# Sixteen tokens of the dense expert layer take fetched rows, and expert matrices move two key blocks at a time

## The chip, the cores and the metric

The kernel runs on one core of a Trainium2 chip. Its time is device microseconds (us) of that core, the median of several runs of one whole launch. A profile of one execution gives the durations. TensorE (PE) does the matrix products, VectorE (DVE) and ScalarE (ACT) the elementwise work, GpSimd (POOL) issues the gathers, SyncE (SP) issues most transfers.

## The reference, cut to what matters

One layer with a token mixer and a channel sublayer, 512 latent tokens of width 1024. The change is in the channel sublayer, a retrieval over 128 x 128 = 16384 experts of one neuron each (8 heads, 16 experts per head and token):

```python
def block(t):                                   # t: 128 tokens
    q = (t @ w_query).reshape(128, 8, 2, 128)
    v1, i1 = top_k(q[:, :, 0] @ k1.T, 16)       # first keys
    v2, i2 = top_k(q[:, :, 1] @ k2.T, 16)       # second keys
    top_s, pos = top_k(all 256 sums v1 + v2, 16)
    idx = take(i1 * 128 + i2, pos)
    g = softmax(top_s)
    act = gelu(einsum('thkd,td->thk', expert_u[idx], t))
    return einsum('thk,thkd->td', g * act, expert_v[idx])
x = layer_norm(ALPHA * x + g2 * y, ln_gamma[1], ln_beta[1])
```

Everything is float32. The kernel writes each float32 factor as a high and a low part and takes three products (`mm3`).

## The kernel before, in words

The mixer comes first and ends at about 490 us. Then class `Peer` treats the 512 tokens in two ways.

Blocks 0 to 2 (384 tokens) are dense. For each of the 128 first keys, `hidden` (L1118) loads the 128 experts of that key as a slice of `uT` (512 KB), splits it into `uh` and `ul` (ACT, DVE), multiplies it with all 384 tokens (24 matmuls with 384 columns, tile `pH`) and takes the GELU. `gated` (L1141) multiplies by the gates, which are zero for experts that were not chosen, and splits the product into `ah` and `al`. `rows` (L1157) loads and splits the slice of `v` (`vh`, `vl`). `combine` (L1161) adds the key's part to the six accumulators `y` (18 matmuls with 512 columns).

Block 3 (128 tokens) is fetched: `fetched` (L1170) gathers per token the rows of `u` and `v` that were chosen, 256 gathers of 512 KB, issued by POOL up to five ahead (`LOOK`). A row of `u` is one DVE instruction with a dot product per token (tile `scr`), a row of `v` one that adds to `yg`.

`run` (L1219) sets the order. In the top stage the queries are made (`pq`), DVE picks the experts (`pick_heads`, `picks`), and gates are built by one-hot products (`gate_block`: DVE tiles `oh` and `ohg`, PE tile `pG`) and written to DRAM (`Gd`). Meanwhile `more` calls `hidden` so that 64 keys are done by the end; 56 of the results go to DRAM (`Hd`). One fetched row stands with each of the 48 gate groups (`ROWS[0]`). In the main stage each step makes `hidden` for one of the other 64 keys and `combine` for one key, with 2.75 fetched rows (`ROWS[1]`). Then `combine` goes on alone. The last five keys (`TAIL`) are held back: their `combine` is done block by block, so that `finish` of a block (DVE: residual and layer norm, L1203) can stand beside the `combine` of the next.

Each engine runs its list in a fixed order, written by a scheduler when the kernel is built; where `manual_schedule` is on, DVE or POOL keeps the order of the source. An instruction that waits holds up all behind it on its engine.

Of the kernel before, what the change touches and what calls it, by code (L numbers as in the profile page):

```python
# [19 lines left out]
D = 1024  # L20
# [11 lines left out]
class Net:  # L32
# [231 lines left out]
    def to_rows(self, js, pool, ps, tag):  # L264
# [4 lines left out]
        r = pool.tile([24, 128], F32, name="mrows")[0:n]  # L269
        nc.scalar.activation(r, p, AF.Copy)  # L270
        nc.gpsimd.dma_start(self.m2d[0, js, :], r)
# [398 lines left out]
    def out_proj(self, pool, mpool, pers, ps, last):  # L670
# [55 lines left out]
        def norms(b):  # L726
# [12 lines left out]
            self.h2[b] = h2  # L739
            for g in range(2):  # L740
# [118 lines left out]

def together(gens):  # L860
# [19 lines left out]
def host_layout(i):  # L880
# [10 lines left out]
    for p in range(2):  # L891
# [20 lines left out]
        "uT": i["peer_u"][0].reshape(128, 128, 8, 128).transpose(0, 3, 2, 1),  # L912
# [5 lines left out]
class Peer:  # L918
# [86 lines left out]
    def picks(self, w, b):  # L1005
# [23 lines left out]
        key = self.key = w.tile([128, 2, 8, 16], F32, name="key")  # L1029
        yield  # L1030
        for s in range(2):
            oh = w.tile(full, BF, name="oh", bufs=2)
# [73 lines left out]
    def load_split(self, rpool, pool, src, tag, bufs=2, far=True, rbufs=2, lbufs=None):  # L1106
        nc = self.nc
        raw = rpool.tile([128, 8, 128], F32, name=tag + "r", bufs=rbufs)
        nc.sync.dma_start(raw, src)
        hi = pool.tile([128, 8, 128], F32R, name=tag + "h", bufs=bufs)  # L1110
        lo = pool.tile([128, 8, 128], F32R, name=tag + "l", bufs=lbufs or bufs)
        nc.scalar.activation(hi, raw, AF.Copy)  # L1112
        eng = nc.gpsimd if far else nc.vector
        sub = eng.tensor_tensor(lo, raw, hi, op=OP.subtract)  # L1114
        if not far:
            self.mark = sub.ins
        return hi, lo

    def hidden(self, n, pool, ring, ps):

        uh, ul = self.load_split(pool, pool, self.a["uT"][n], "u", 3, False, 3, 2)
        p = ps.tile([128, self.TD], F32, name="pH")
        for k in range(8):
            self.n.mm3(p, uh[:, k, :], ul[:, k, :], self.hh[:, k, :self.TD], self.hl[:, k, :self.TD], k == 0, k == 7)
        kept = not self.AHEAD <= n < self.AHEAD + self.SPILL
        r = ring.tile([128, self.TD], F32, name="gel" if kept else "gels", bufs=self.AHEAD + 1 if kept else 3)
        act = self.nc.scalar.activation(r, p, AF.Gelu_apprx_tanh)  # L1127
        if kept:
            self.gel[n] = r
        else:  # L1130
            self.nc.sync.dma_start(self.Hd[n - self.AHEAD], r)
        return act

    def back(self, n, ring):

        if self.AHEAD <= n < self.AHEAD + self.SPILL:
            r = self.gel[n] = ring.tile([128, self.TD], F32, name="gel", bufs=self.AHEAD + 1)
            self.nc.sync.dma_start(r, self.Hd[n - self.AHEAD])

    def gated(self, n, pool, vpool, bufs, mark=None):  # L1140

        nc = self.nc
        NG = self.TD // self.GT
        if n % self.GN == 0:
            self.Gn = pool.tile([128, NG, self.GN, self.GT], F32, name="Gn", bufs=2)
            nc.sync.dma_start(self.Gn, self.Gd[:, :, n:n + self.GN, :].rearrange("g m n t -> m g n t"))
        g = self.gel.pop(n)
        g3 = g.rearrange("p (g t) -> p g t", t=self.GT)
        with self.tc.issue_after(mark) if mark else ExitStack():
            nc.vector.tensor_tensor(g3, g3, self.Gn[:, :, n % self.GN, :], op=OP.mult)  # L1150
        ah = vpool.tile([128, self.TD], F32R, name="ah", bufs=bufs)
        al = vpool.tile([128, self.TD], F32R, name="al", bufs=bufs)
# [4 lines left out]
    def rows(self, n, pool, vpool, bufs, far=False, rbufs=2):  # L1157

        return self.load_split(pool, vpool, self.a["v"][n * 128:(n + 1) * 128].rearrange("e (k c) -> e k c", k=8), "v", bufs, far, rbufs)

    def combine(self, n, b, ops, halves=(0, 1)):  # L1161
# [236 lines left out]
```

## Time and profile before

| | |
|---|---|
| Runs | 1752.32, 1756.19, 1761.13 us; median 1756.19 |
| The profiled execution | 1752.71 us, of it 1750.9 us between first and last instruction |
| Busy share | PE 97%, DVE 83%, ACT 47%, POOL 24% |
| `pH` matmuls | 3 x 1024, 384 columns |
| `y` matmuls | 3 x 768, 512 columns |
| Granted TensorE clock | 0.987 of full speed |

How to read it: a matmul's own duration (some 340 or 395 ns) is longer than its distance to the next, since matmuls overlap in the pipeline, so the cost of one is read from the distance between starts. The mean busy shares run over stages with different limits; the rows below are by stage.

### The profile page before, as it was taken

To read this page: it belongs to the slowest core of one execution; us is meant where nothing else is said; L and a number is where in the kernel's file an instruction comes from. 1 tells how busy PE (TensorE), PEld (TensorE's weight loads), DVE (VectorE), ACT (ScalarE), POOL (GpSimd) and SP (SyncE) were. 2 spreads that over 40 slices of the span, in tenths; PEclk is the share of its full clock that TensorE was granted. 3 is DMA by queue.
4 is the path that set the end of the run, shared out by engine and by line. 5 is a ranking of instruction groups with operands and counts; after the bars stand their busy time and mean duration, and the time that the engine had idled before them with its cause. 6 is when DMAs were issued, how large, how long until landed. Compare 5 with 4: busy or idle time off the path is not lost. (4 is left out here: it accounts for less than half of the span.)

```text
span 1750.9 us, 28102 instructions
## 1 busy us (share of the span) xinstructions
PE 1692.9 (97%) x10440; PEld 1477.1 (84%) x10440; DVE 1446.2 (83%) x2917; ACT 829.9 (47%) x1412; POOL 416.6 (24%) x294
## 2 busy tenths in 40 slices
PE   6999999989999999999999999999999999999996
PEld 3888777877788999999998999999999998888884
DVE  6689888877989999999996887877877786777767
ACT  4667677655233356676663333333333333333341
POOL 0000000000033012258323454443444442111000
PEclk8999999989999999999999999999999999999998
DMA  8345445143322358989999999989989989999852
GB/s 318 127 145 163 130 142 183 53 158 135 133 74 72 97 172 304 332 298 311 347 332 364 374 338 329 334 304 332 333 301 336 326 287 333 336 347 282 275 194 96
DMA packets 175499, 431.10 MB, mean 246 GB/s; under 512 B 15137, under 2 KB 78977, under 8 KB 171266
## 3 DMA queue, kind: packets, MB, share of 16 engines
q1 hardware_dynamic: 137234, 290.87, 48.8%
q0 software_dynamic: 37552, 136.35, 22.3%
q8 instruction: 81, 1.33, 0.3%
q10 hardware_dynamic: 576, 2.10, 0.3%
q14 instruction: 56, 0.46, 0.1%
HBM read 380.48 MB, written 48.78 MB: 245 GB/s over the span
## 5 line engine op out<-in xcount | busy, mean ns | idle before, releaser
L139 PE MATMUL pH<-hh,uh 128*128 128x384 f32 x1024 | 350.1, 342 | 1.0 <-ACT gels L1127 1.0
L141 PE MATMUL pH<-hh,ul 128*128 128x384 f32 x1024 | 347.7, 340 | 1.6 <-DVE ul L1114 1.6
L140 PE MATMUL pH<-hl,uh 128*128 128x384 f32 x1024 | 346.9, 339 | 0.0
L139 PE MATMUL y<-vh,ah 128*128 128x512 f32 x768 | 302.5, 395 | 2.6 <-ACT ah L1153 2.6
L141 PE MATMUL y<-vh,al 128*128 128x512 f32 x768 | 301.8, 395 | 0.0
L140 PE MATMUL y<-vl,ah 128*128 128x512 f32 x768 | 301.4, 392 | 0.0
L1114 DVE TENSOR_TENSOR vl<-vr,vh 128x1024 fp32r<-128x1024 f32 x128 | 156.7, 1224 | 152.4 <-ACT vh L1112 152.0
L1183 POOL DMA_INDIRECT erow<-in_u_dram,ix x128 | 189.6, 1481 | 368.7 <-DVE scr L1192 214.6
L1183 POOL DMA_INDIRECT erow<-in_v_dram,ix x128 | 188.9, 1476 | 323.8 <-DVE yg L1200 181.1
L1112 ACT ACTIVATE vh<-vr 128x1024 fp32r<-128x1024 f32 x128 | 135.1, 1057 | 199.8 <-issue 128.8
L1153 ACT ACTIVATE ah<-gel 128x384 fp32r<-128x384 f32 x128 | 66.8, 524 | 272.7 <-DVE gel L1150 267.9
L139 PEld LDWEIGHTS pH<-hh,uh 128*128 128x128 f32 x1024 | 192.3, 188 | 3.9 <-ACT gels L1127 1.4
L140 PEld LDWEIGHTS pH<-hl,uh 128*128 128x128 f32 x1024 | 192.7, 188 | 2.7
L141 PEld LDWEIGHTS pH<-hh,ul 128*128 128x128 f32 x1024 | 192.3, 188 | 2.6 <-DVE ul L1114 2.4
L1112 ACT ACTIVATE uh<-ur 128x1024 fp32r<-128x1024 f32 x128 | 135.0, 1056 | 117.6 <-PE pH L140 71.2
L141 PEld LDWEIGHTS y<-vh,al 128*128 128x128 f32 x768 | 144.7, 188 | 34.4
L139 PEld LDWEIGHTS y<-vh,ah 128*128 128x128 f32 x768 | 144.4, 188 | 33.3 <-ACT ah L1153 2.9
L140 PEld LDWEIGHTS y<-vl,ah 128*128 128x128 f32 x768 | 144.5, 188 | 30.6
L1114 DVE TENSOR_TENSOR ul<-ur,uh 128x1024 fp32r<-128x1024 f32 x128 | 156.0, 1219 | 16.5 <-PE pH L141 13.6
L1200 DVE SCALAR_TENSOR_TENSOR yg<-erow,act,yg 128x1024 f32<-128x1024 f32 x127 | 162.4, 1279 | 0.1
L1192 DVE SCALAR_TENSOR_TENSOR scr<-erow,h 128x1024 bf16<-128x1024 f32 x128 | 156.1, 1219 | 0.0
L139 PE MATMUL pc<-hTh,wh 128*128 128x512 f32 (+1 forms) x304 | 109.5, 360 | 0.3 <-ACT G L379 0.3
(381 smaller groups left out, 3033.8 us busy)
## 6 DMA issues: line engine op xcount, KB each, us to landing
ur<-in_uT_dram SPq DMA_DIRECT2D x128, 512.0 KB
vr<-in_v_dram SPq DMA_DIRECT2D x128, 512.0 KB
Gd<-stage SPq DMA_DIRECT2D x24, 1024.0 KB
Gn<-Gd SPq DMA_DIRECT2D x16, 1536.0 KB
wraw<-in_w_cf_dram SPq DMA_DIRECT2D x24, 512.0 KB
wada<-in_w_ada_dram SPq DMA_DIRECT2D x48, 256.0 KB
Hd<-gels SPq DMA_DIRECT2D x56, 192.0 KB
gel<-Hd SPq DMA_DIRECT2D x56, 192.0 KB
```

What stands on the lines that cost most here:

```text
L139: mm(out, lh, rh, start=start, stop=False)
L140: mm(out, lh, rl, start=False, stop=False)
L141: mm(out, ll, rh, start=False, stop=stop)
L1112: nc.scalar.activation(hi, raw, AF.Copy)
L1114: sub = eng.tensor_tensor(lo, raw, hi, op=OP.subtract)
L1153: nc.scalar.activation(ah, g, AF.Copy)
L1183: nc.gpsimd.indirect_dma_start(out=e, out_offset=None, in_=a[src], in_offset=bass.IndirectOffsetOnAxis(ap=self.ix[:, j:j + 1], axis=0))
L1192: nc.vector.scalar_tensor_tensor(scr, e, 1.0, h2, op0=OP.mult, op1=OP.mult, accum_out=dots[:, j:j + 1])
L1200: nc.vector.scalar_tensor_tensor(y, e, act[:, j:j + 1], y, op0=OP.mult, op1=OP.add)
```

## The change

Five parts. (1) The dense product with `u` leaves out the last 16 of the 384 tokens (`SH`, `TU` = 368), so `pH` matmuls have 368 columns. (2) For these 16 tokens the dot products come from fetched rows: the 16 tokens x 128 chosen experts are spread over 128 partitions, 16 more gathers with index `ixs`, each with one DVE instruction (`sdots`). The GELU of the dots is multiplied into the gates of the 16 tokens, before the gate groups of block 2 are built, so that the gate matrix itself holds gate times activation and `gated` copies it. To have the indices in time `picks` of block 2 moves ahead of that of block 3. (3) `hidden`, `gated`, `rows` and `back` take two first keys at a time: loads of 1 MB, 8 KB in a row per partition, where there were 512 KB with 4 KB. (4) Buffers follow: `TAIL` is two pairs, `AHEAD` four pairs, `finish` holds its two tiles as one. (5) Fetched rows are done from `picks` of block 3 on; `ROWS[2]` is 0.75, counted twice per pair.

The diff, cut to its core:

```diff
+            if b == 2:
+                nc.gpsimd.dma_start(self.h2d, h2[128 - Peer.SH:128, :])
...
-        "uT": i["peer_u"][0].reshape(128, 128, 8, 128).transpose(0, 3, 2, 1),
+        "uT": i["peer_u"][0].reshape(64, 2, 128, 8, 128).transpose(0, 4, 1, 3, 2),
+        "vd": i["peer_v"][0].reshape(64, 2, 128, 8, 128).transpose(0, 2, 1, 3, 4),
...
+    SH = 16
+    TU = TD - SH
-    AHEAD = 8
-    SPILL = 56
+    AHEAD = 4
+    SPILL = 28
-    ROWS = (1.0, 2.75, 0.6)
+    ROWS = (1.0, 2.75, 0.75)
-    TAIL = 5
+    TAIL = 2
...
+    def load_split(self, pool, src, tag, bufs):
+        raw = pool.tile([128, 2, 8, 128], F32, name=tag + "r", bufs=2)
         nc.sync.dma_start(raw, src)
+        for e in range(2):
+            hi, lo = (pool.tile([128, 8, 128], F32R, name=tag + i, bufs=bufs) for i in "hl")
+            nc.scalar.activation(hi, raw[:, e], AF.Copy)
+            self.mark = nc.vector.tensor_tensor(lo, raw[:, e], hi, op=OP.subtract).ins
...
     def hidden(self, n, pool, ring, ps):
-        uh, ul = self.load_split(pool, pool, self.a["uT"][n], "u", 3, False, 3, 2)
-        p = ps.tile([128, self.TD], F32, name="pH")
-        for k in range(8):
-            self.n.mm3(p, uh[:, k, :], ul[:, k, :], self.hh[:, k, :self.TD], self.hl[:, k, :self.TD], k == 0, k == 7)
+        u = self.load_split(pool, self.a["uT"][n], "u", 3)
+        for e in range(2):
+            uh, ul = u[e]
+            p = ps.tile([128, TU], F32, name="pH")
+            for k in range(8):
+                self.n.mm3(p, uh[:, k, :], ul[:, k, :], self.hh[:, k, :TU], self.hl[:, k, :TU], k == 0, k == 7)
+            self.nc.scalar.activation(r[:, e, :TU], p, AF.Gelu_apprx_tanh)
...
+        nc.scalar.activation(g4[:, :, NU:], gates[:, :, NU:], AF.Copy)
         with self.tc.issue_after(mark) if mark else ExitStack():
-            nc.vector.tensor_tensor(g3, g3, self.Gn[:, :, n % self.GN, :], op=OP.mult)
+            nc.vector.tensor_tensor(g4[:, :, :NU], g4[:, :, :NU], gates[:, :, :NU], op=OP.mult)
+        ah = vpool.tile([128, 2, self.TD], F32R, name="ah", bufs=bufs)
+        al = vpool.tile([128, 2, self.TD], F32R, name="al", bufs=bufs)
...
+        order = [("s", j) for j in range(SH)]
+        order += [(src, j) for j0 in range(0, 128, 16) for src in "uv" for j in range(j0, j0 + 16)]
...
+            if src == "s":
+                nc.vector.scalar_tensor_tensor(e, e, 1.0, y, op0=OP.mult, op1=OP.mult, accum_out=sdots[:, j:j + 1])
+                if j == SH - 1:
+                    nc.scalar.activation(sdots, sdots, AF.Gelu_apprx_tanh)
+                    for q in range(128 // SH):
+                        nc.scalar.dma_start(act[128 - SH:128, q * SH:(q + 1) * SH], sdots[q * SH:(q + 1) * SH, :])
+            elif src == "u":
+                nc.vector.scalar_tensor_tensor(e, e, 1.0, h2, op0=OP.mult, op1=OP.mult, accum_out=dots[:, j:j + 1])
+                if j == 15:
+                    g = self.g[96:128, 2].rearrange("p h k -> p (h k)")
+                    nc.vector.tensor_tensor(g, g, act[96:128], op=OP.mult)
...
-        x1, r = (ring.tile([128, 8, 128], F32, name="vr", bufs=4).rearrange("p k c -> p (k c)") for _ in range(2))
+        two = ring.tile([128, 2, 8, 128], F32, name="vr", bufs=2)
+        x1, r = (two[:, i].rearrange("p k c -> p (k c)") for i in range(2))
...
+                for i, _ in enumerate(self.picks(w, 2)):
+                    if i % 2:
+                        more(0.5)
+                index()
...
+                choice.enter_context(tc.manual_schedule(engines={mybir.EngineType.DVE, mybir.EngineType.Pool}))
+                for q in range(128 // SH):
+                    nc.gpsimd.dma_start(yg[q * SH:(q + 1) * SH, :], n.h2d)
+                for q in range(128 // SH):
+                    nc.gpsimd.dma_start(self.ixs[q * SH:(q + 1) * SH, :], self.ix[128 - SH:128, q * SH:(q + 1) * SH])
+                fetched = self.fetched(fp, fp, yg)
+                next(fetched)
                 for i, _ in enumerate(self.picks(w, 3)):
                     if i % 2:
-                        more(1)
+                        more(0.5)
+                    if i > 1:
+                        next(fetched)
+                index()
...
                     for i, _ in enumerate(self.picks(w, 0)):
                         if i % 2:
-                            more(1)
+                            more(0.5)
+                        fetch(1)
...
-                for i, m in enumerate(seq[:128 - self.TAIL]):
-                    fetch(self.ROWS[1] if nh < 128 else self.ROWS[2])
+                for i, m in enumerate(seq[:64 - self.TAIL]):
+                    rate = self.ROWS[1] if nh < 64 else self.ROWS[2]
+                    fetch(rate)
...
+                    fetch(rate)
+                    v = self.rows(m, pools[i % len(pools)])
```

What stands in an engine's list, at three places. First DVE where the indices of the first fetched rows are made, before (`ix` of block 3; `oh`, `key`, `prf` belong to `picks`, `sm` and `gp` to the softmax):

```order
L1279 SCALAR_TENSOR_TENSOR ix<-key 128x128
L1001 TENSOR_REDUCE sm<-gp 128x32
L1114 TENSOR_TENSOR ul<-ur,uh 128x1024
L1002 RECIPROCAL sm<-sm 128x32
L1037 TENSOR_TENSOR oh<-oh 128x8x128
L1003 TENSOR_TENSOR gp<-gp,sm 128x512
L1037 TENSOR_TENSOR oh<-oh 128x8x64
L1033 TENSOR_TENSOR oh<-prf,iota_5232 128x2048
L1114 TENSOR_TENSOR ul<-ur,uh 128x1024
L1037 TENSOR_TENSOR oh<-oh 128x8x32
L1035 TENSOR_TENSOR oh<-oh,spread 128x2048
L1038 TENSOR_TENSOR key<-oh 128x128
```

And now, from the second row after `ix` of block 2 on (`sdots` is the dot product of the first added row):

```order
L1018 TENSOR_REDUCE sm<-gp 128x32
L1135 TENSOR_TENSOR ul<-ur,uh 128x1024
L1019 RECIPROCAL sm<-sm 128x32
L1052 TENSOR_TENSOR oh<-prf,iota_5231 128x2048
L1020 TENSOR_TENSOR gp<-gp,sm 128x512
L1040 CAST pf<-pr 128x512
L1041 CAST pf<-pos_5221 128x128
L1030 TENSOR_SCALAR pr<-pos_5224 128x128
L1044 SCALAR_TENSOR_TENSOR pf<-pf 128x128
L1030 TENSOR_SCALAR pr<-pos_5224 128x128 x3
L1221 SCALAR_TENSOR_TENSOR erow,sdots<-erow,yg 128x1024
L1054 TENSOR_TENSOR oh<-oh,spread 128x2048
```

Before, 28 rows with five `ul` among them stood between `ix` and the first fetched row; now it is 11 rows with one. The next `ul` comes after three fetched rows.

Second POOL, from the casts of the constants to the gathers, before:

```order
L276 DMA sc_4721<-m2d 128x1024
L1267 CAST iota_5232<-iota_row 128x256
L1268 CAST iota_5233<-iota_row 128x256
L961 TENSOR_TENSOR wql<-wqr,wqh 128x1024 x13
L1183 DMA erow<-in_u_dram,ix 128x1024 x16
```

And now (`h2d` holds the 16 tokens, `yg` their copies for eight groups of partitions, `ixs` the 16 indices of each partition):

```order
L741 DMA h2d<-h_5015 16x1024
L1306 CAST iota_5231<-iota_row 128x256
L1307 CAST iota_5232<-iota_row 128x256
L978 TENSOR_TENSOR wql<-wqr,wqh 128x1024 x2
L1334 DMA yg<-h2d 16x1024 x2
L978 TENSOR_TENSOR wql<-wqr,wqh 128x1024
L1334 DMA yg<-h2d 16x1024 x4
L978 TENSOR_TENSOR wql<-wqr,wqh 128x1024
L1334 DMA yg<-h2d 16x1024 x2
L978 TENSOR_TENSOR wql<-wqr,wqh 128x1024 x9
L1336 DMA ixs<-ix 16x16 x8
L1212 DMA erow<-in_u_dram,ixs 128x1024 x16
```

Eight copies of the tokens stand among the splits of the query weights, and eight small transfers ahead of the first gather.

Third ACT at the end of the last steps, before (`mrows` is the row of the modulation that `finish` needs):

```order
L1112 ACTIVATE vh<-vr 128x1024
L1153 ACTIVATE ah<-gel 128x384
L270 ACTIVATE mrows<-prow 8x128
L1359 ACT_TABLE_LOAD
L127 ACTIVATE rsz<-mvz,eps 128x1
```

And now (`q_4773` is the memory that `mrows` and `rsz` share):

```order
L1134 ACTIVATE vh<-vr 128x1024 x2
L1174 ACTIVATE gel<-Gn 128x2x16
L1179 ACTIVATE ah<-gel 128x768
L270 ACTIVATE q_4773<-prow 8x128
L1424 ACT_TABLE_LOAD
L127 ACTIVATE q_4773<-q_4773,eps 128x1
```

The row still comes behind the last split of `v`; the `ah` between is twice as long.

## Rows read from the trace of the kernel before

**Rows 1.** Section 2 of the page, the span in 40 slices, tenths busy.

```profile
PE   6999999989999999999999999999999999999996
DVE  6689888877989999999996887877877786777767
```

**Rows 2.** Windows by stage: stretch, its length, busy per engine, clock, DMA share, GB/s.

```profile
489.30:915.80 426.50, 422.94 (x3057) 395.68 (x3058) 418.63 (x1282) 239.55 (x467) 148.82 (x67) 1.00 0.69 237
915.80:941.70 25.90, 23.37 (x157) 22.89 (x154) 13.21 (x14) 9.46 (x16) 5.28 (x4) 1.00 1.03 357
941.70:1461.50 519.80, 519.77 (x2597) 472.31 (x2598) 408.68 (x510) 182.21 (x254) 225.80 (x173) 1.00 0.94 329
1461.50:1713.60 252.10, 252.10 (x1083) 202.79 (x1083) 184.14 (x253) 94.51 (x126) 29.80 (x26) 1.00 0.86 285
1713.60:1750.90 37.30, 21.14 (x92) 16.82 (x90) 27.26 (x46) 4.90 (x12) 1.15 (x2) 0.83 0.31 109
```

**Rows 3.** Timeline of PE, main stage: start, length, instruction.

```profile
1097.97 0.35 PE L139 MATMUL pH<-hh,uh 128*128 128x384 f32 x1
...
1102.21 0.40 PE L139 MATMUL y<-vh,ah 128*128 128x512 f32 x1
...
1106.33 0.35 PE L139 MATMUL pH<-hh,uh 128*128 128x384 f32 x1
```

**Rows 4.** Timeline of PE, projections with 256 columns in the mixer.

```profile
163.21 0.28 PE L141 MATMUL pc<-hTh,wl 128*128 128x256 f32 x1
...
165.11 0.28 PE L139 MATMUL pc<-hTh,wh 128*128 128x256 f32 x1
```

**Rows 5.** Timeline of DVE, the first pick and the last gate group.

```profile
489.30 0.86 DVE L944 MAX8 v<-yg 128x8 f32<-128x128 f32 x4
...
915.41 0.42 DVE L1085 TENSOR_TENSOR ohg<-oh,gp 128x512 bf16<-128x512 bf16 x1
```

**Rows 6.** Groups by line, DVE, 489.3 to 915.8: busy, mean ns, idle before.

```profile
L1114 DVE TENSOR_TENSOR ul<-ur,uh 128x1024 fp32r<-128x1024 f32 x63 | 76.6, 1216 | 7.7 <-PE pH L141 4.8 <-issue 2.2 <-ACT uh L1112 0.6
...
L1192 DVE SCALAR_TENSOR_TENSOR scr<-erow,h 128x1024 bf16<-128x1024 f32 x32 | 39.0, 1218 | 0.0
...
L1200 DVE SCALAR_TENSOR_TENSOR yg<-erow,act,yg 128x1024 f32<-128x1024 f32 x15 | 19.1, 1274 | 0.0
```

**Rows 7.** Timeline of POOL: a small transfer and the first gather.

```profile
133.73 0.58 POOL L276 DMA_DIRECT2D g<-m2d  x1 [1.29 <-DMA m2d<-mrows]
...
650.53 1.03 POOL L1183 DMA_INDIRECT erow<-in_u_dram,ix  x1 [82.68 <-DVE ix L1279]
```

**Rows 8.** Timelines of DVE and POOL, the last pick on `yg` and the third split.

```profile
496.51 0.86 DVE L944 MAX8 v<-yg 128x8 f32<-128x128 f32 x4
...
501.15 2.38 POOL L961 TENSOR_TENSOR wql<-wqr,wqh 128x1024 fp32r<-128x1024 f32 x1 [3.09 <-ACT wqh L959]
```

**Rows 9.** Timeline of PE, from the top stage into the main stage.

```profile
938.84 0.34 PE L141 MATMUL pH<-hh,ul 128*128 128x384 f32 x1
941.73 0.49 PE L139 MATMUL y<-vh,ah 128*128 128x512 f32 x1 [2.56 <-ACT ah L1153]
```

**Rows 10.** Timelines of PE, ACT, POOL and DVE over the end, in order of time.

```profile
1713.63 0.47 PE L139 MATMUL y<-vh,ah 128*128 128x512 f32 x1
...
1713.85 1.06 ACT L1112 ACTIVATE vh<-vr 128x1024 fp32r<-128x1024 f32 x1 [2.73 <-issue]
1714.81 0.51 ACT L1153 ACTIVATE ah<-gel 128x384 fp32r<-128x384 f32 x1
...
1718.32 0.57 POOL L276 DMA_DIRECT2D Gn<-m2d  x1 [1.97 <-DMA m2d<-mrows]
...
1721.97 1.29 DVE L1211 TENSOR_TENSOR vr<-yg,Gn 128x512 f32<-128x512 f32 x2 [5.33 <-DMA Gn<-m2d]
...
1734.34 0.40 PE L141 MATMUL y<-vh,al 128*128 128x512 f32 x1
...
1746.20 1.41 DVE L135 SCALAR_TENSOR_TENSOR vr<-vr,rsz,Gn 128x512 f32<-128x512 f32 x2
```

More of the change, by code (lines that the diff above doesn't have):

```diff
@@ L1155, in gated, with rows, combine @@
         return ah, al
-    def rows(self, n, pool, vpool, bufs, far=False, rbufs=2):
-        return self.load_split(pool, vpool, self.a["v"][n * 128:(n + 1) * 128].rearrange("e (k c) -> e k c", k=8), "v", bufs, far, rbufs)
-    def combine(self, n, b, ops, halves=(0, 1)):
+    def rows(self, n, pool):
+        return self.load_split(pool, self.a["vd"][n], "v", 2)
+    def combine(self, n, e, b, ops, halves=(0, 1)):
         (ah, al), v = ops
@@ L1250, in more @@
                 def more(count):
-                    nonlocal nh
-                    for _ in range(count):
+                    nonlocal nh, asked
+                    asked += count
+                    while nh + 1 <= asked:
                         self.hidden(nh, up, gl, hps)
@@ L1309, in run @@
                             fetch(self.ROWS[0])
-                            more(first + (out_to - first) * at // groups - nh)
+                            more(first + (out_to - first) * at / groups - asked)
                         for _ in following:
@@ L1330, in run @@
                             vp = deep.enter_context(tc.tile_pool(name="vring", bufs=1, side="right", reuse_waits="tile"))
+                            pools.append(vp)
                             g2 = n.mods_last(vp)
                     else:
-                        v = self.rows(m, vp, vp, 3, rbufs=4)
-                        if i % 2:
-                            next(g2, None)
-                    if nh == 128 and i + ahead < 128:
+                        next(g2, None)
+                    fetch(rate)
+                    v = self.rows(m, pools[i % len(pools)])
+                    if nh == 64 and i + ahead < 64:
                         self.back(seq[i + ahead], gl)
                     ops = self.gated(m, w, w, self.TAIL, mark), v
-                    for b in range(ND):
-                        self.combine(m, b, ops)
+                    for e in range(2):
+                        for b in range(ND):
+                            self.combine(2 * m, e, b, ops)
                 fetch(256)
@@ L1360, in run @@
                 rows = [rows[:, i] for i in range(3)]
-                self.finish(3, (yg[:, :512], yg[:, 512:]), w, vp, rows, out)
+                bits = Bits(n.q0[1][:, 128:])
+                self.finish(3, (yg[:, :512], yg[:, 512:]), bits, vp, rows, out)
                 for b in range(ND):
@@ L1364, in run @@
                         for i, a_, v in zip(tail, acts, vs):
-                            self.combine(i, b, (a_, v), (hf,))
-                    self.finish(b, self.y[b], w, vp, rows, out)
+                            for e in range(2):
+                                self.combine(2 * i, e, b, (a_, v), (hf,))
+                    self.finish(b, self.y[b], bits, vp, rows, out)
 def build(tc, a, out):
@@ L1378, in build @@
         n.m2d = dp.tile([1, 32, 128], F32, name="m2d")
+        n.h2d = dp.tile([Peer.SH, D], F32, name="h2d")
         n.mixer(es)
```

124 lines of the change are left out of this document (63 added, 61 removed).

## The prediction

> **What bounds the kernel now.** I read the busy shares by slices first, then windows by stage, then the timeline of the engine that is full in each stage. The slices [rows 1] show PE at nine tenths or more nearly throughout; DVE is as full from slice 13 to 21 and falls to seven or eight tenths after it. So I cut the span at the first pick on DVE (489.3), the end of the last gate group (915.8) [rows 5], the first `y` matmul (941.7), the last `pH` (1461.5) and the first held-back `y` matmul (1713.6) [rows 2].
>
> In the top stage, 489.3 to 915.8, DVE is busy 418.6 of 426.5 us (98%) and PE 422.9. The reader is to see that both are full, and that DVE stood only 7.9 us, 4.8 of them for PE to free a buffer of `ul` [rows 2, 6]. In the main stage, 519.8 us, PE never stops and DVE has 111 us free; in the stage of `combine` alone, 252.1 us, it is the same. So a shorter matmul pays in full in the main stage, but in the top stage only as far as DVE lets it. At the end neither is full: PE is done at 1734.7 (its last row plus length), and a chain of DVE work runs to 1747.6 [rows 10].
>
> **What 16 columns are worth.** In the main stage 24 `pH` matmuls with 384 columns take 1102.21 - 1097.97 = 4.24 us, 176.7 ns each, and 18 `y` matmuls with 512 take 4.12 us, 228.9 ns each [rows 3]. Sixteen matmuls with 256 columns take 165.11 - 163.21 = 1.90 us, 118.8 ns each [rows 4]. The slope is 0.45 ns per column from 256 to 384 and 0.41 from 384 to 512; 16 columns less give 6.5 to 7.2 ns, and I take 6.8. Over all 3072 such matmuls that is 20.9 us.
>
> The Trainium skill (TensorE: Matmul & The Clock Gate, Back-to-back issue gap) says that in a stream of weight loads and matmuls both set the distance between matmuls, and it gives 81 ns for 128 columns and 131 ns for 512. By that slope, 0.13 ns per column, 16 columns would be worth 2.1 ns, by an estimate from that page's figures, and all 3072 matmuls 6.4 us. The trace does not agree so far: its three sizes lie nearly on one line with more than three times that slope.
>
> **Top stage.** PE gains 6.8 ns on some 64 x 24 matmuls, 10.4 us. DVE does not gain. Fetched rows in it rise from 48 to 58 (the 4 beside `picks` of block 3, 6 beside `picks` of block 0, 48 with the gate groups), and one `ul` fewer stands before the last gate group (62 for 63). A row is 1.22 us [rows 6], of which the next instruction covers some 0.08, so ten rows less one `ul` add about 11 us: 418.6 becomes 429.6. The rows of `u` are now written as float32; the additions to `yg`, which are too, take 1.27 in place of 1.22 [rows 6], so at most 3 us more on 58 rows; I put the difference down to the factor that the addition reads, and take none.
>
> To that comes a wait. DVE now keeps the order of the source, and the first added row stands 11 instructions behind `ix`. Ahead of its data lie eight small transfers on POOL at 0.58 us each, 1.3 until the last has landed [rows 7], and the gather itself. No row shows one landing; the nearest is another 512 KB through POOL, from 1718.32 to the DVE work that waits for it at 1721.97, 3.65 us [rows 10]. That is 4.6 + 1.3 + 3.7 = 9.6 us, and I take 11 with the gaps between issues. The 11 instructions in between are one `ul` and one `oh` at 1.2 each and small ones, some 5 us together. So DVE stands 6 us; I keep 0 and 12 as ends (a gather that lands early, rows behind it that come late too). Behind that row wait two `oh` chains, two more fetched rows and then the next `ul`, so PE runs out of split weights there. Of the idle time of before, the 4.8 us for PE go, since PE is ahead now, and 3.1 stay.
>
> The last gate group then ends at 489.3 + 429.6 + 6 + 3.1 = 928.0, against 915.8. From there PE needs two us for its last gate products and 139 matmuls of `pH` at 169.9 ns, 23.6 us, until the first `y`: 953.6, against 941.7. (Before, that `y` waited for `ah`, 2.6 us [rows 9], at the end of a chain through `Gd` and `Gn` that takes 26 us from the last gate group; PE now needs as long, so this wait is at most shifted.) PE has then done 67.8 keys instead of 67, worth 3.4 us. The top stage loses 953.6 - 941.7 - 3.4 = 8.5 us. Ends: with no DVE idle at all the last group is at 918.9, a loss of -0.6; with 7.9 of idle, 12 of waiting and 3 for the wider write, 941.8, a loss of 22.
>
> The eight copies of the tokens cost nothing: the first waits until `yg` is read as scores, the pick on it begins at 496.51 and its last reading is some 3 us later, and the third split of query weights does not start before 501.15 [rows 8]; two issues at 0.58 fit in between. Without that cover the split, and a query behind it, would be late by the same 1 to 2 us once.
>
> **Main stage.** 60.2 keys are left, 60.2 x 24 x 6.8 ns = 9.8 us gained (9.4 to 10.4). DVE has the room: per pair 5.5 rows, two `ul`, two `vl` and the longer gate products come to 13 us of 16.4. Loads of 8 KB per partition can only help a DMA share of 0.94 for which PE does not wait [rows 2], so I take nothing for them. At the end of this stage the pools change hands, and the first pair of `v` in the new pool must follow the last `uh`; before, that pair of buffers was in a pool of its own. I take 1 us (0 to 4).
>
> **End.** The held-back work falls from five keys to four. The row that `finish` needs comes behind the last split of `v`, which waits for the last not held-back `combine`. So `finish` starts 8.3 us after the first held-back matmul (1713.63 to 1721.97), four of them run one after another, and the span ends 37.3 us after that matmul [rows 2, 10], whatever PE does: PE has 21 us of it. With one key less held back that matmul comes 18 x 0.229 = 4.1 us later, and the `ah` ahead of the row is some 0.4 us longer. `finish` also holds its two tiles as one, so the third must wait for the first's output to leave before it loads `x1`; DVE has 12.6 us of `finish` work in between, so 0 to 2. Together 5 us lost (3 to 7).
>
> **Sum.** +8.5 - 9.8 + 1 + 5 = +4.7 us on the profiled execution of 1752.7, so 1757.4. The median of the runs lies 3.5 above that execution; the median after is then 1756.2 + 4.7 = 1761. Of 20.9 us that PE gains, 10 vanish behind DVE in the top stage. Differences under 0.5% (8.8 us, so 1747.4 to 1765.0) are no change that a measurement can tell.
>
> **Rivals.**
>
> B, slower: DVE waits for fetched rows more than once. Fourteen added rows stand within some 45 us among the picks; each new gather can only be issued when a row is used, and lands some 4.7 us later (1.03 to issue, 3.65 to land). If three or four of them are late by 2 to 3 us, the wait is 14 us in place of 6, and with the wider write's 3 us the sum is 1772. For it: every us of DVE is on the path there. Against it: five gathers are ahead. It decides from 10 us of idle time on DVE ahead of L1221.
>
> C, faster: PE sets the top stage, not DVE. Then the 10.4 us there count, the first wait is hidden by splits already made, and the sum is -20.9 + 1 + 5 = -15, 1741. For it: PE was busy 422.9 there too, and DVE did wait for PE. Against: DVE stood 7.9 us only, and gets 11 more.
>
> D, slower: a matmul is not shorter with fewer columns, because the weight loads (busy 472 of 519.8 us in the main stage [rows 2]) set the distance. Then the main stage gains nothing, 1761 + 9.8 = 1771. Against it the matmuls with 256 columns, 118.8 ns apart with the same weight load. The page's rule named above would stand between this and the forecast: 3 us gained in the main stage by an estimate from its figures.
>
> **Chances.** Forecast 0.56 (0.50 within 0.5%, 0.06 above it), B 0.24 (0.22 slower, 0.02 same), C 0.15 (faster), D 0.05 (slower). Faster 0.15, same 0.52, slower 0.33. The forecast's own range from its ends is 1753 to 1769; to hold eight of ten it must take in most of B and the near edge of C, where part of the top stage gains: 1746 to 1776.
>
> **What would show it.** `pH` starts 168 to 171 ns apart in the main stage; 176 would be D. The last gate group at 925 to 932, with DVE standing 3 to 9 us ahead of the first L1221, and PE idle around it; a last group at or before 916 is C, after 936 B. The main stage some 10 us shorter per 64 keys. From the first held-back matmul to the end 37 to 39 us. The forecast is wrong if PE still has no gaps in the top stage, or if the stretch behind 1461 grows by more than the end costs.

## The result, and the profile after

The changed kernel takes 1776.32 us (median of 4 runs, 1775.77 to 1778.75), the kernel before 1758.2 beside it (4 runs): a ratio of 1.011, interval 1.008 to 1.014. It is 1.1% slower: the forecast of 1761 was 15 us too low, and the end of its range, 1776, was passed by 0.3. The profiled execution took 1778.75 us, 1776.8 of it between first and last instruction, 25.9 more than before. The medians lie only 18.1 apart: the profiled execution of before is 5.5 us under the median beside it, the one after 2.4 over. So some 8 us of the differences by stage below belong to the two executions.

Windows by stage after, cut at the same events as [rows 2] (first pick, end of the last gate group, first `y`, last `pH`, first held-back `y`, end); the columns are those of [rows 2]:

```profile
488.60:941.20 452.60, 421.02 (x3043) 393.93 (x3043) 430.24 (x1304) 241.28 (x466) 150.50 (x93) 0.96 0.67 234
941.20:973.60 32.40, 27.90 (x189) 27.25 (x187) 19.37 (x26) 13.44 (x23) 8.95 (x6) 0.95 1.03 373
973.60:1471.80 498.20, 494.99 (x2560) 450.37 (x2561) 396.17 (x439) 177.40 (x250) 261.89 (x170) 1.00 0.93 337
1471.80:1737.40 265.60, 256.47 (x1119) 210.26 (x1118) 182.58 (x197) 94.35 (x122) 54.28 (x32) 0.99 0.81 280
1737.40:1776.80 39.40, 16.90 (x74) 13.31 (x72) 27.89 (x46) 5.45 (x13) 1.17 (x2) 0.76 0.30 107
```

| stage | length before to after | difference | by the prediction's terms |
|---|---|---|---|
| first pick to first `y` (two rows above) | 452.4 to 485.0 | +32.6 | +11.9 |
| main stage | 519.8 to 498.2 | -21.6 | -13.2 |
| `combine` alone | 252.1 to 265.6 | +13.5 | +5.1 |
| end | 37.3 to 39.4 | +2.1 | +0.9 |

(The right column cuts the forecast's terms at the same events: 3.4 us of keys done early move from the first stage to the second, 4.1 us of a key less held back stand in the third.) With 0.7 us less ahead of the first pick the differences give the 25.9. One more shift is not in the forecast: as a step now makes two keys, 62 keys of `combine` fall into the main stage and 62 behind it, where it was 63 and 60, and only one of these two keys is held back less. So 4.1 us of the third row's excess come out of the second row.

**Shorter matmuls.** Timeline of PE, main stage after, as [rows 3]:

```profile
1157.62 0.33 PE L139 MATMUL pH<-hh,uh 128*128 128x368 f32 x1
...
1165.57 0.40 PE L139 MATMUL y<-vh,ah 128*128 128x512 f32 x1
...
1173.74 0.33 PE L139 MATMUL pH<-hh,uh 128*128 128x368 f32 x1
```

Two keys lie between, so 48 `pH` take 7.95 us, 165.6 ns each, and 36 `y` 8.17 us, 226.9 each; before 176.7 and 228.9. A `pH` matmul is 11.1 ns shorter, where 6.8 were predicted.

**The first fetched row.** Timelines of POOL, DVE and PE where `ixs` is made and the first added row is used; brackets give idle time and what ended it:

```profile
644.82 3.89 POOL L1336 DMA_DIRECT2D ixs<-ix  x8 [77.72 <-issue]
654.09 1.03 POOL L1212 DMA_INDIRECT erow<-in_u_dram,ixs  x1 [5.38 <-PE pH L141]
```

```profile
659.27 1.23 DVE L1221 SCALAR_TENSOR_TENSOR erow<-erow,yg 128x1024 f32<-128x1024 f32 x1 [9.78 <-DMA erow<-in_u_dram,ixs]
...
670.18 2.35 DVE L1135 TENSOR_TENSOR ul<-ur,uh 128x1024 fp32r<-128x1024 f32 x2
```

```profile
655.35 0.33 PE L140 MATMUL pH<-hl,uh 128*128 128x368 f32 x1
671.45 0.68 PE L141 MATMUL pH<-hh,ul 128*128 128x368 f32 x1 [15.78 <-DVE ul L1135]
671.92 0.51 PE L139 MATMUL pH<-hh,uh 128*128 128x368 f32 x1
672.23 0.51 PE L140 MATMUL pH<-hl,uh 128*128 128x368 f32 x1
...
676.20 0.33 PE L141 MATMUL pH<-hh,ul 128*128 128x368 f32 x1
```

The gather waits for all eight transfers of `ixs`; PE, named in the bracket, is only the last event near (in e3 and e8 below the same wait, 5.44 and 4.89 us, names `ixs`). DVE stands 9.78 us, and the `ul` that PE needs is behind that row, two more rows and two `oh` chains, 10.9 us later still. PE stands 15.8 us. From 655.30 to 676.00 the mean granted clock is 0.59, where it was 1.00 before (windows as above, before and after), and behind the gap the matmuls are 0.31 us apart instead of 0.17, at the lower level of 1.2 GHz, until 676.2.

```profile
655.30:676.00 20.70, 20.70 (x120) 20.67 (x120) 20.02 (x35) 11.79 (x14) 6.25 (x6) 1.00 0.91 332
```

```profile
655.30:676.00 20.70, 4.92 (x17) 4.62 (x17) 16.59 (x29) 3.82 (x2) 10.98 (x9) 0.59 0.84 281
```

PE's gap is not a price of its own: up to the last gate group PE makes 62.0 keys in both kernels, as the lists say, and the stage ends where DVE's list does. Its length is DVE's work, 430.2 us, and DVE's idle time, 22.4: the 9.8 above and 12.6 elsewhere. Of the latter 3.2 stand right behind a single late load of `ur`, and 2.2 more ten us later, for which the profile names no releaser (ACT and DVE):

```profile
866.81 1.06 ACT L1134 ACTIVATE uh<-ur 128x1024 fp32r<-128x1024 f32 x1 [6.32 <-DMA ur<-in_uT_dram]
867.90 1.23 DVE L1135 TENSOR_TENSOR ul<-ur,uh 128x1024 fp32r<-128x1024 f32 x1 [2.80 <-ACT uh L1134]
869.58 0.29 DVE L1075 CAST gp<-pkT 128x128 bf16<-128x128 f32 x1 [0.45 <-ACT kT L1070]
879.42 1.23 DVE L1093 TENSOR_TENSOR oh<-iota,kT 128x2048 bf16<-128x2048 bf16 x1 [2.20 <-issue]
```

**The first `y`.** SP's queue and what waits for it on ACT and PE, after (`Gd` are the gates in DRAM, `Gn` the first load of them, 1536 KB):

```profile
944.97 0.32 SPq L1121 DMA_DIRECT2D Gd<-stage  x1
...
953.98 0.37 SPq L1130 DMA_DIRECT2D vr<-in_vd_dram  x1
955.28 0.38 SPq L1169 DMA_DIRECT2D Gn<-Gd  x1
```

```profile
971.71 0.23 ACT L1174 ACTIVATE gel<-Gn 128x32 f32<-128x32 f32 x1 [2.35 <-DMA Gn<-Gd]
```

```profile
973.62 0.50 PE L139 MATMUL y<-vh,ah 128*128 128x512 f32 x1 [2.19 <-ACT ah L1179]
```

The gates are used 16.4 us after their load is issued. Before it was 8.8 (SP and DVE):

```profile
931.79 0.38 SPq L1146 DMA_DIRECT2D Gn<-Gd  x1
```

```profile
940.57 0.55 DVE L1150 TENSOR_TENSOR gel<-gel,Gn 128x384 f32<-128x384 f32 x1
```

PE stands 2.3 us for a buffer of `pH` and 2.2 for this `ah`, and once more 2.4 at 1030.9, behind the next load of gates.

**The handover.** SP, ACT and PE at the end of the main stage, after:

```profile
1466.63 0.33 SPq L1130 DMA_DIRECT2D vr<-in_vd_dram  x1
```

```profile
1476.69 2.00 ACT L1134 ACTIVATE vh<-vr 128x1024 fp32r<-128x1024 f32 x2 [4.03 <-DMA vr<-in_vd_dram]
```

```profile
1477.80 1.22 PE L139 MATMUL y<-vh,ah 128*128 128x512 f32 x2 [5.66 <-ACT vh L1134]
```

The first pair of `v` in the new pool is asked for 5 us before the last `pH` (1471.8) and PE waits for it 5.7 us; nothing waited there before ([rows 2], busy 252.10 of 252.10).

### The profile page after: what moved, and what is told of

Read it like the earlier page. It is cut to its first block, busy times and chain, and to the rows that moved or that the text cites. A ratio compares the mean times of both kernels' runs of the same rounds, so it can differ in the third digit from the quotient of the medians.

```text
span 1776.8 us, 27590 instructions
## 1 busy us (share of the span) xinstructions
PE 1669.0 (94%) x10440; PEld 1460.4 (82%) x10440; DVE 1450.7 (82%) x2824; ACT 831.2 (47%) x1413; POOL 483.1 (27%) x327
## 5 line engine op out<-in xcount | busy, mean ns | idle before, releaser
L141 PE MATMUL pH<-hh,ul 128*128 128x368 f32 x1024 | 342.7, 336 | 22.2 <-DVE ul L1135 22.1
L139 PE MATMUL pH<-hh,uh 128*128 128x368 f32 x1024 | 344.1, 336 | 5.7 <-ACT gel L1153 4.7
L140 PE MATMUL pH<-hl,uh 128*128 128x368 f32 x1024 | 341.3, 333 | 0.0
L1212 POOL DMA_INDIRECT erow<-in_v_dram,ix x128 | 218.4, 1706 | 239.0 <-DVE yg L1239 133.6
L1212 POOL DMA_INDIRECT erow<-in_u_dram,ix x128 | 197.3, 1541 | 311.3 <-DVE erow L1227 178.6
L141 PEld LDWEIGHTS y<-vh,al 128*128 128x128 f32 x768 | 144.6, 188 | 33.2 <-DVE al L1180 2.9
L1239 DVE SCALAR_TENSOR_TENSOR yg<-erow,q,yg 128x1024 f32<-128x1024 f32 x127 | 162.4, 1278 | 0.3
L1227 DVE SCALAR_TENSOR_TENSOR erow<-erow,h 128x1024 f32<-128x1024 f32 x128 | 151.9, 1217 | 0.1
L1180 DVE TENSOR_TENSOR al<-gel,ah 128x768 fp32r<-128x768 f32 x64 | 61.0, 954 | 72.3 <-ACT ah L1179 72.1
```

What stands on the lines that cost most here:

```text
L139: mm(out, lh, rh, start=start, stop=False)
L140: mm(out, lh, rl, start=False, stop=False)
L141: mm(out, ll, rh, start=False, stop=stop)
L1180: nc.vector.tensor_tensor(al, g, ah, op=OP.subtract)
L1212: nc.gpsimd.indirect_dma_start(out=e, out_offset=None, in_=a["v" if src == "v" else "u"], in_offset=bass.IndirectOffsetOnAxis(ap=ix[:, j:j ...
L1227: nc.vector.scalar_tensor_tensor(e, e, 1.0, h2, op0=OP.mult, op1=OP.mult, accum_out=dots[:, j:j + 1])
```

## The experiments

Ratios are to the kernel before on the same chip. Each edit is to the changed kernel. The times by stage come from one profiled execution each, which lies between 6.4 us under (e1) and 2.4 over (e8) the median of its runs: a difference of a few us between two of them is shown only where a wait in the trace goes with it.

| | ratio, interval | last gate group | first `y` | last `pH` | first held-back `y` | span |
|---|---|---|---|---|---|---|
| before | | 915.8 | 941.7 | 1461.5 | 1713.6 | 1750.9 |
| changed | 1.011 [1.008, 1.014] | 941.2 | 973.6 | 1471.8 | 1737.4 | 1776.8 |
| e1, rows later | 1.0032 [1.001, 1.0053] | 919.8 | 954.6 | 1450.0 | 1716.6 | 1756.3 |
| e2, pairs alone | 1.0029 [1.001, 1.0048] | 910.4 | 939.7 | 1455.0 | 1717.4 | 1757.4 |
| e3, 384 columns | 1.0169 [1.0146, 1.0193] | 936.7 | 968.0 | 1483.4 | 1751.4 | 1791.4 |
| e4, handover | 1.0056 [1.0037, 1.0076] | 931.5 | 965.0 | 1465.3 | 1727.6 | 1765.4 |
| e5, half loads | 1.0129 [1.01, 1.0157] | 934.1 | 962.5 | 1462.3 | 1731.3 | 1771.4 |
| e6, no late rows | 1.0149 [1.0124, 1.0173] | 930.0 | 964.0 | 1464.1 | 1740.8 | 1780.3 |
| e7, combined | 1.007 [1.0046, 1.0093] | 916.4 | 944.7 | 1451.2 | 1723.0 | 1761.2 |
| e8, first step clear | 1.0054 [1.0032, 1.0076] | 935.9 | 969.1 | 1464.1 | 1728.9 | 1768.6 |
| e9, all mended | 0.9934 [0.9909, 0.9959] | 908.8 | 938.2 | 1437.9 | 1708.1 | 1747.7 |
| e10, mended, no tokens | 1.0001 [0.9986, 1.0015] | 901.1 | 932.8 | 1447.2 | 1714.1 | 1753.8 |

**e1: the first fetched rows later.** Beside the picks of block 3:

```diff
-                    if i > 1:
-                        next(fetched)
```

> The changed kernel, without the four added fetched rows beside the picks of block 3 (they come later, beside the picks of block 0 and the gate groups; everything is still computed). Theory A (DVE's fixed order): DVE stood 9.8 us for the first gathered row, PE ran dry for 16 us behind it and got half the clock for 17 us; with the first row later the gather has landed, so this wait goes to under 2 us, DVE also has four rows (4.6 us) less before the last gate group, and that group ends at 924 to 928 instead of 941; total 1776 - 14 to 18 = 1758 to 1762. Rival B (two keys at a time make DVE's list so uneven that PE runs dry anyway): the wait goes, PE still stands elsewhere, total 1771 or more.

Measured 1764.51 us, above A's range and below B's. The stage up to the last gate group is 433.5 us long instead of 452.6, with 425.2 us of work on DVE; the first row finds its data, and the waits for added rows are these two (DVE):

```profile
664.41 1.23 DVE L1221 SCALAR_TENSOR_TENSOR erow<-erow,yg 128x1024 f32<-128x1024 f32 x1 [1.92 <-DMA erow<-in_u_dram,ixs]
...
669.79 1.23 DVE L1221 SCALAR_TENSOR_TENSOR erow<-erow,yg 128x1024 f32<-128x1024 f32 x1 [1.27 <-DMA erow<-in_u_dram,ixs]
```

Of these 19 us 5 are the four rows themselves, the other 14 idle time on DVE (22.4 us in the changed kernel, 8.3 here). Not all of that is the wait's: e3, e4, e5 and e8, which leave this order as it is, have the stage 444.8 to 445.5 us long, with waits of 8.7 to 11.0 us for the first row and 5 to 6 us of other idle time. Against these the misplaced rows cost 11 to 12 us, their own 5 among them. The other 7 to 8 us of the changed kernel's 452.6 are in none of these four, and the late load of `ur` above gives 3 to 5.5 of them (the longest such wait of ACT in the second half of this stage is 3.0 in e3, e4, e5 and e8). Whether other executions of the changed kernel have it is not known; the three others took 2.2 to 3.0 us less. What e1 still loses to the kernel before is elsewhere.

**e2: pairs alone.** No 16 tokens: 384 columns, no added rows, the order of picks as before.

```diff
-    TU = TD - SH
+    TU = TD
...
-        order = [("s", j) for j in range(SH)]
-        order += [(src, j) for j0 in range(0, 128, 16) for src in "uv" for j in range(j0, j0 + 16)]
+        order = [(src, j) for j0 in range(0, 128, 16) for src in "uv" for j in range(j0, j0 + 16)]
...
```

> Two keys at a time alone: 384 dense tokens, no added fetched rows, picks in the order of the kernel before; loads, buffers and tail as changed. Theory A: top stage as before (last gate group at 915 to 920, no gap of PE over 3 us), the handover wait of 6 us and the shorter tail (+5 us) stay; if the matmuls' shorter distances (166 ns for 368 columns, 227 for 512, where 170 and 229 were expected) come from the pairs, pH is at 173 and y at 227 ns, and the total is 1748 to 1758. Rival B: the uneven list costs in the top stage, last gate group later than 925, total 1765 or more.

Measured 1765.16 us, B's time, but not at B's place: the last gate group is at 910.4, earlier than A said. Pairs alone cost 0.3%. The matmuls do not: `pH` stays at 176 ns and `y` is at 227 (PE, main stage, two keys of `y`):

```profile
1106.60 0.40 PE L139 MATMUL y<-vh,ah 128*128 128x512 f32 x1
...
1114.77 0.34 PE L139 MATMUL pH<-hh,uh 128*128 128x384 f32 x1
```

PE waits at the first `y` and 4.9 us at the handover:

```profile
939.74 0.79 PE L139 MATMUL y<-vh,ah 128*128 128x512 f32 x1 [5.06 <-ACT ah L1176]
```

**e3: the price of 16 columns.** All 384 columns are computed and the last 16 left unused:

```diff
-            p = ps.tile([128, TU], F32, name="pH")
+            p = ps.tile([128, self.TD], F32, name="pH")
...
```

> The changed kernel with 384 columns in every pH matmul again (the last 16 are computed and not used). Columns decide: pH 173 to 177 ns apart instead of 166, main stage longer by 60 x 24 x 7 to 10 ns = 10 to 15 us, top stage nearly the same since DVE sets it: total 1786 to 1792. Rival (the distance is set by the weight load or by the transfers, not by columns): pH stays under 169 ns, total 1775 to 1780.

Measured 1791.2 us, as the first theory said. Timeline of PE: 48 `pH` take 8.43 us, 175.6 ns each, so 16 columns are worth 10.0 ns.

```profile
1209.58 0.34 PE L139 MATMUL pH<-hh,uh 128*128 128x384 f32 x1
...
1218.01 0.40 PE L139 MATMUL y<-vh,ah 128*128 128x512 f32 x1
```

**e4: the handover.** The two pools of `v` are exchanged, so the first pair behind the last `pH` stays in the pool already in use:

```diff
-                    v = self.rows(m, pools[i % len(pools)])
+                    v = self.rows(m, pools[(i + 1) % len(pools)])
...
```

> The changed kernel with the two pools of v in the other order from the 32nd pair on, so that the pair beside the last pH uses the pool that is already there. Theory A: the wait of 6.0 us of y for vh at 1471.8, the small ones behind it and the 6.8 us at half clock go, total 1776 - 7 to 10 = 1766 to 1769. Rival: the new pool's first load is as late for the next pair, the wait moves there, total 1774 or more.

Measured 1770.34 us, between the two. The wait at the handover is 3.0 us in place of 5.7, and one pair later:

```profile
1476.84 2.93 PE L139 MATMUL y<-vh,ah 128*128 128x512 f32 x6 [3.01 <-ACT vh L1134]
```

This is worth less than the ratios differ (0.5%); in the profiled executions the rest lies in the first stage, 444.9 us here, which the edit does not touch.

**e5: half loads.** Two transfers of 512 KB for each pair, so packets of 4 KB:

```diff
-        nc.sync.dma_start(raw, src)
+        for e in range(2):
+            nc.sync.dma_start(raw[:, e], src[:, e])
```

> The changed kernel with each load of a pair of keys issued as two transfers of 512 KB (4 KB in a row per partition), so the packets are those of before; buffers and order stay. Theory A (8 KB packets and joint loads do nothing for TensorE, the loss lies in the order of DVE's work): y matmuls stay 226 to 228 ns apart in the main stage, the first y stays 30 to 34 us behind the last gate group, 1774 to 1780 us. Rival P (large loads crowd out the load of the gates, which is in pieces of 512 bytes and lands 16 us after its issue where it took 9 before): the gates land 9 to 12 us after their issue, the first y comes 26 to 28 us behind the last gate group, 1768 to 1772 us. Rival Q (the 8 KB packets are why y went from 229 to 227 ns): 229 to 233 ns, 1780 to 1786 us.

Measured 1775.4 us. `y` stays at 226.9 ns, so packets of 8 KB are not what made it shorter (Q falls); the gates still land 15.3 us after their issue (P falls). The first `y` does come only 28.4 us behind the last gate group, but because PE makes 4.6 keys there in place of 5.8.

**e6: no late rows.**

```diff
-                            fetch(self.ROWS[0])
+                            fetch(self.ROWS[0] if b < 2 else 0.0)
...
-    ROWS = (1.0, 2.75, 0.75)
+    ROWS = (1.0, 2.75, 0.9)
```

> The changed kernel without fetched rows beside the gate groups of block 2 (16 rows fewer in the top stage, done later: 0.9 in place of 0.75 per step in the stage of combine alone). Theory T (between the last gate group and the first y the DMA engines are full, share 1.03, and a gather beside every step makes the first loads of v and the gates late): the last gate group ends at 933 to 938, the first y comes 25 to 28 us behind it, 1764 to 1769 us. Rival D (the wait is a chain of fixed length through the loads of a pair, whatever the gathers do): still 31 to 34 us between them, 1769 to 1774 us. Rival E (those rows cost nothing in the top stage because DVE waits there anyway): last gate group at 940 to 942, 1774 to 1778 us.

Measured 1781.68 us. The stretch is D's, 34.0 us, but no theory had the time. The last gate group came 11 us earlier; then (PE, first `y` and handover):

```profile
964.01 0.79 PE L139 MATMUL y<-vh,ah 128*128 128x512 f32 x1 [9.61 <-ACT ah L1179]
...
1475.47 1.22 PE L139 MATMUL y<-vh,ah 128*128 128x512 f32 x2 [11.06 <-ACT vh L1134]
```

What DVE saved, PE spent waiting for the gates, and the handover, where rows are now denser, waits 11 us.

**e7: combined.** The edits of e1, e4 and e6 with `ROWS = (0.82, 2.85, 0.97)`.

> Three edits together: no fetched rows beside the picks of block 3, the pools of v exchanged at the handover, and 0.82 rows per gate group in blocks 0 and 1, none in block 2 (32 rows in the top stage in place of 58, the others later: rates 2.85 and 0.97). If the losses add up (12 us for the first, 6 for the second, 10 to 13 for the third): 1744 to 1752 us, faster than before; the last gate group at 905 to 912, the first y at 934 to 940, no stretch of 16 us in which TensorE stands. Rival (the moved rows come back as a cost in the main stage, where the DMA engines are at 0.93 already): TensorE gets gaps behind the first y and y spacing above 229 ns, 1755 to 1762 us.

Measured 1766.44 us, beyond both ranges and by its ratio no better than e1 alone. The rival was right that the cost returns, not that `y` gets longer (227 ns). PE waits for gates at the first `y`, for the next gates in the main stage, and at the handover:

```profile
944.73 0.50 PE L139 MATMUL y<-vh,ah 128*128 128x512 f32 x1 [3.91 <-ACT ah L1179]
...
1009.79 0.68 PE L139 MATMUL pH<-hh,uh 128*128 128x368 f32 x1 [4.64 <-ACT gel L1153]
...
1466.90 2.93 PE L139 MATMUL y<-vh,ah 128*128 128x512 f32 x6 [7.23 <-ACT vh L1134]
```

**e8: the first step clear.**

```diff
-                    rate = self.ROWS[1] if nh < 64 else self.ROWS[2]
+                    rate = 0.0 if i == 0 else self.ROWS[1] if nh < 64 else self.ROWS[2]
```

> The changed kernel without fetched rows in the first step of the main stage (the rates of the other steps stay, so the rows slip by one step). In the changed kernel the first gates land 16 us after their issue, in the kernel before 8, and rows used there start new gathers at the same time. Theory G (gathers started behind the last gate group crowd out the load of the gates): the gates land 8 to 11 us after their issue, the first y comes 26 to 28 us behind the last gate group in place of 32.4, 1769 to 1773 us. Rival F (the load waits for the pairs' own transfers of 1 MB and for the gates to reach the memory, gathers play no part): the gates land 14 to 17 us after their issue, the first y stays 31 to 34 us behind, 1774 to 1779 us.

Measured 1767.89 us. The gates landed 15.8 us after their issue and the first `y` came 33.2 us behind the last gate group, as F said; the time was shorter than both ranges, since the first stage took 444.8 us and the main stage had no wait. But neither e6 nor e8 took all gathers away: one left the rows of the first step, the other those beside the gate groups.

What then sets the landing? The DMA view of the stretch from the issue of the first gate load until its last piece of 512 bytes has come shows the bytes that all queues moved; q0 are the gathers. Before (7.6 us), after (15.6 us) and e9 below (8.1 us):

```profile
DMA packets 3410, 2.52 MB, mean 332 GB/s; under 512 B 55, under 2 KB 3209, under 8 KB 3410
...
q1 hardware_dynamic: 3410, 2.52, 109.6%
```

```profile
DMA packets 4005, 5.80 MB, mean 372 GB/s; under 512 B 123, under 2 KB 3184, under 8 KB 3756
...
q1 hardware_dynamic: 3500, 3.98, 78.8%
q0 software_dynamic: 505, 1.82, 28.9%
```

```profile
DMA packets 3310, 2.65 MB, mean 327 GB/s; under 512 B 39, under 2 KB 3111, under 8 KB 3216
...
q1 hardware_dynamic: 3309, 2.64, 107.5%
```

In the other runs: 3.40 MB in 10.6 us (e7), 3.86 in 11.8 (e2), 5.51 in 15.3 (e5), 5.52 in 15.8 (e8), 5.66 in 16.9 (e6), 6.21 in 16.7 (e1). The load itself is 1.57 MB. All nine lie at 0.32 to 0.37 MB per us, but where the engines are full any stretch moves about that much, so this alone does not show what delays the load. Two things show more. First, no gathers fall into this stretch in the kernel before, in e9 and in e10 (2.41 MB in 7.5 us); in all other runs 1.05 to 2.47 MB of them do, and the load takes 10.6 us or more. Second, the order of the packets. In the changed kernel no 512-byte piece of the load moves in the first 5.8 us (the view from 955.28 to 961.10; the 60 packets under 2 KB are those under 512 B):

```profile
DMA packets 548, 2.42 MB, mean 416 GB/s; under 512 B 60, under 2 KB 60, under 8 KB 409
```

What moves are gathers and the loads that SP had issued before: `ur` at 950.46, `Hd` at 953.56, `vr` at 953.98. Before, the first piece moved 1.3 us after the issue, in e8 3.9, in e6 1.2; in these last two most of the load had moved when gathers came and stretched the rest. So bytes ahead of the load in SP's queue and gathers beside it both delay it; how much of the 8 us is due to each, no run shows. The Trainium skill (DMA: Bandwidth & Descriptors, Specifications) lists about 358 GB/s as the memory's limit for one core; the stretches here moved 320 to 372 GB/s, so that figure is near but not a ceiling in this case.

**e9: all mended.** The edits of e1 and e8, and:

```diff
-                    v = self.rows(m, pools[i % len(pools)])
+                    v = self.rows(m, pools[i % 2 if i > 31 else 0])
...
-                            fetch(self.ROWS[0])
-                            more(first + (out_to - first) * at / groups - asked)
+                            fetch(self.ROWS[0] if b < 2 else 0.6)
+                            more(first + (out_to - 1 - first) * at / groups - asked)
...
+                    more(out_to - asked)
...
-    ROWS = (1.0, 2.75, 0.75)
+    ROWS = (0.82, 2.85, 0.9)
```

> All places mended at once: no fetched rows beside the picks of block 3; 0.82 rows per gate group in blocks 0 and 1 and 0.6 in block 2; the last pair of keys of the top stage made behind the gate groups; no rows in the first step of the main stage; the first two steps after the last pH take v through the pool that they already use, and only then the new one; rates 2.85 and 0.9 later. Theory A (the gain of the shorter pH is there, 15 us, and was lost at the wait for the first added row, at the first y and at the handover): last gate group at 905 to 915, first y 26 to 29 us behind it, the wait at the handover under 2 us, 1743 to 1752 us, faster than before. Rival (what is saved at one place returns at the next because the DMA engines are full there): the waits for the gates or for v reappear with 4 us or more each, 1756 to 1764 us.

Measured 1748.33 us, A's time: 0.7% faster than the kernel before. Its windows by stage, cut as above:

```profile
490.40:908.80 418.40, 403.19 (x2981) 375.94 (x2982) 409.60 (x1276) 238.02 (x459) 106.08 (x76) 1.00 0.66 231
908.80:938.20 29.40, 29.40 (x209) 29.25 (x208) 17.57 (x17) 15.81 (x28) 6.40 (x3) 1.00 0.93 312
938.20:1437.90 499.70, 499.70 (x2604) 455.87 (x2603) 402.65 (x457) 179.99 (x251) 276.26 (x177) 1.00 0.95 342
1437.90:1708.10 270.20, 259.65 (x1120) 210.81 (x1119) 197.53 (x216) 94.02 (x124) 86.90 (x46) 0.99 0.88 311
```

PE is busy through all of the second and third row: no wait at the first `y`, none in the main stage. The third mend, the handover, did less: the wait for `v` is gone, but 1.5 us for `vl` and 3.8 us for `ah` stand ahead of 1452 and 1460, and the stage of `combine` alone is the longest of all here except e7 and e6. Several edits were made at once, so what each gives is not shown.

**e10: mended, without the 16 tokens.** e2 with the edits of e8 and the pool, `more` and `ROWS = (0.6, 2.85, 0.9)`.

> The kernel with all places mended, but without the 16 tokens: 384 columns, no added rows, 0.6 rows per gate group in all blocks (the constraint that 32 rows are done before block 2 is gone). It tells whether the columns themselves pay once their rows are out of the way. Theory A (they pay): pH 176 ns apart in place of 166, 31 us more of TensorE's time on 3072 matmuls, less what the 16 added rows and their transfers cost in the top stage, some 15: 1756 to 1768 us. Rival (the rows cost as much as the columns give, and the gain came from pairs and mended places alone): 1744 to 1752 us.

Measured 1756.33 us, at the near end of A, a ratio of 1.0001 to the kernel before. So the 0.7% that e9 gains come with the tokens, and pairs bring nothing by themselves, as far as these two runs compare: they also differ in rows per gate group.

## Why the prediction was wrong

Two steps failed, both between first pick and first `y`, where the forecast's +11.9 became +32.6: the idle time that DVE gets, which was taken too small, and the wait ahead of the first `y`, which was put at nothing.

1. *"So DVE stands 6 us ... and 3.1 stay."* The stage up to the last gate group took 452.6 us, 13.9 more than the forecast's 438.7. DVE's work was right, 430.2 us against 429.6; its idle time was 22.4 where 9.1 were taken. The place of the first wait was right, its size was not. The 1.3 us until the last small transfer has landed, taken from one wait of [rows 7], measured 5.4 (issues end at 648.71, first gather at 654.09), and the gather 5.2 in place of 3.65 (to 659.27); the issues took 3.9, not 4.6. The chain is 14.5 us where I took 11, and the wait 9.8 (8.7 to 11.0 in the runs with the same order). The larger part is the other idle time, 12.6 where I let 3.1 stay: 3 to 5.5 of it stand behind one late load of `ur`, which no term of mine allowed for. In e3, e4, e5 and e8 this other idle time was 5 to 6, so some 7 us of it may be the profiled execution's. That PE "runs out of split weights there" came true (15.8 us), and needed no price beside DVE's.

2. *"This wait is at most shifted"*: 25.6 us from last gate group to first `y` became 32.4, 4.5 of it with PE idle. I counted PE's work and took the chain through `Gd` and `Gn` as fixed. It is not: the load of the gates shares DMA engines that were full already, share 1.03 in that row of [rows 2], which I had shown and not used. With loads ahead of it and gathers beside it, it took twice as long; e1 to e8 had 28.3 to 34.8 us here, and in e9, with no gathers in the stretch, the load landed in 8.1 us again and PE had no wait.

3. *Main stage, -9.8.* Right in sign, too small; with 3.4 of keys done early it was -13.2 against -21.6. 16 columns are 10.0 ns (e3), above the 6.5 to 7.2 worked out from steps of 128 columns; the slope between 368 and 384 is 0.63 ns per column. Still further off is 0.13, the estimate from the figures that the Trainium skill (TensorE: Matmul & The Clock Gate, Back-to-back issue gap) gives for 128 and 512 columns. The main stage also lost a key of `y` to the next stage (4.1 us), and waits of 3.2 us went against it. `y` went from 229 to 227 ns, and from 233 to 227 in the stage of `combine` alone; e2 and e5 show that it comes with pairs and not with columns or packets. What in the pairs does it stays open.

4. *Handover, 1 (0 to 4).* Measured 5.7 us; 62 keys at 226.9 ns per `y` are 253.2 us, so 12.4 of the stage's 265.6 are lost: 9.1 with PE idle (5.7 here, the others shorter waits for `al` and `ah`), the rest mostly in matmuls at the lower clock behind the wait, 0.43 us apart until 1481.8. I said that the first pair must follow the last `uh`; that it is also loaded only then, 1 MB beside the loads of `Gn` and `Hd`, I did not price. That this contention is what spoils e7 and e6 at the same place fits their denser rows but is not shown alone.

5. *End, +5.* One key later, 4.1, and 39.4 us from the first held-back matmul, 0.4 above the band.

The range was also narrower than its own ends. A loss of 22 us in the top stage, which the prediction names as an end, gives 1774.5 by itself, and with the ends of the other terms 1780; "1753 to 1769" has no working. The measured last gate group, 941.2, is at that end (941.8), though not by its terms.

Of the rivals, B came nearest: the place, almost its bound (10 us ahead of L1221; 9.8 came), its mark for the last gate group (after 936) and a time of 1772. But it wanted several waits for fetched rows; there was one, and the rest was idle time of other kinds. C fell, as the last gate group did not end by 916, D with 166 ns.

## What to carry to other kernels

Find the engine whose list ends the stage and add up its work and all its idle time; a longer gap on another engine (here 15.8 us on PE behind 9.8 on DVE) can look worse and cost nothing beyond it. Where a stage begins with a load, look at what its DMA engines carry between issue and landing: loads already in the same queue and gathers beside it. If their share is 1 already, whatever is added there is likely to make the load later. A shorter matmul can be worth its price (here 0.7%), but only once rows and loads are moved off those two places.

## What the runs showed of the hardware

- A gather behind eight small transfers started 4.9 to 6.0 us after the last of them was issued (e8 4.89, changed 5.38, e5 5.96); 1.3 us, from one transfer in [rows 7], was far too low.
- 16 columns fewer, 384 to 368, made a matmul 10.0 ns shorter, 0.63 ns per column (e3 and changed), where 256 to 384 gives 0.45 ([rows 3, 4]).
- After PE had stood 15.8 us, its granted clock was at the lower level in 14 further matmuls, 0.31 us apart; 14 times 0.14 us, this cost only some 2 us.
- A load of 1.57 MB in pieces of 512 bytes landed in 7.5 to 8.1 us with no gathers in that time (before, e9, e10) and in 10.6 to 16.9 us with 1.05 to 2.47 MB of them.
